# Small matmuls on opposite halves or blocks of the array, issued alternately instead of in blocks

## The chip, the core and the metric

The kernel runs as one program on one core of a Trainium2 chip. The metric is the device time of one execution in microseconds. The kernel before has a median of 2231.14 us over three runs (2227.08 to 2231.18).

The engines of the core are called PE (TensorE, matrix products), DVE (VectorE), ACT (ScalarE), POOL (GpSimd) and SP (SyncE, which here only issues DMAs). A product on PE is a weight load (the stationary operand) and a matmul that streams the other operand through. An fp32 product shows up in the trace as two weight loads and two matmul instructions.

## The reference

A sequence of 256 tokens of width 1024 goes through two blocks.

```python
# first block
x = x + 0.5 * swiglu(rms_norm(x), ffn1)            # hidden width 2816
x = x + token_mixer(rms_norm(x))                   # three attention branches, gated, then w_out
x = x + 0.5 * swiglu(rms_norm(x), ffn2)
# second block
ctx_states = rwkv_context_states(h_ctx @ w_in)     # only the final states of the recurrence
mixed = (g_hy * hyena(cols) @ hy_proj + g_rw * rwkv(cols, ctx_states) @ rw_proj) @ w_out
x = x + gate1 * rmsnorm(mixed)
x = x + gate2 * rmsnorm(expert_choice_moe(h2))     # 16 experts of width 2048, 32 tokens each
```

The recurrence is RWKV-7 with 8 heads of 64, run once forward and once backward in time:

```python
def step(S, inp):
    sa = einsum('bhij,bhj->bhi', S, a_t)
    S = S * w_t[:, :, None, :] + sa[..., None] * b_t[:, :, None, :] + v_t[..., None] * k_t[:, :, None, :]
    y = einsum('bhij,bhj->bhi', S, r_t)
```

The first of the attention branches (A) has 12 heads of 64 in 3 groups of 4; head h of the three groups shares one softmax. The third (C) selects keys by an index score, a sum over 8 small heads of relu(q . k) times a weight.

## The kernel before, in words

**Products.** The weights of the projections are split in two parts (`wsplit`: line 245 on ACT makes the high part, line 246 on DVE the low part, lines 270 to 272 do it in three engines for part of the second mixer), and each projection is three fp32r products per block (lines 287 to 289, 299 to 302, 345 to 349). The small products, which the change is about, are fp32 and not split.

**Order.** Nothing orders PE's stream by hand around the change. The kernel is traced as straight code; a planner with a model of the engines then lays out each engine's instructions, earlier code first among what it holds to be ready, and hands out the buffers of the tile pools. A read and a write of the same PSUM bank are kept apart in the order of the source. Each engine then runs its instructions in that fixed order. PSUM is split in `psM` (4 banks), `psT` (2, tiles named `tr`) and `psX` (2, tiles named `px`).

**Two halves.** A tensor with a contraction of 64 sits on partitions 0 to 63 or 64 to 127, and a product on it uses the upper or the lower half of the array's rows; an output that goes to partitions 0 to 63 or 64 to 127 uses one half of its columns.

**The recurrence** (`rwkv`, lines 921 to 1247) is called twice: by `context_states` for the context (final states only, while the first FFN and the attention's projections run) and by `mixer2` for the tokens (while the Hyena branch and the gates run). It treats chunks of 64 tokens.

- `elementwise(n, d, t)`, four times per call (direction d, token tile t): two low-rank products into a psX bank each, line 1010 on rows 0 to 63 of `up` and line 1017 on rows 64 to 127, four of 64x128 each, each bank followed by four tanh on ACT (1013, 1020).
- `products(d, t)`: line 1076 (into psX, masked by DVE line 1078), lines 1095 and 1098, whose loop alternates the row halves with each head, and line 1106, four products of `kt` and `vt` for each of the two chunk halves `cc`, each into its own psT bank, followed by copies on ACT (1110).
- The inverses of unit triangular 32-blocks are made on DVE (1131 to 1133) and travel through DRAM (`sc2`, `TC`). Then the off-diagonal blocks: lines 1162 and 1170, 64 products of 32x32 each, ordered block by block (two directions times two chunks); the second reads the copy `Bs` of the first's bank.
- The steps (lines 1197 to 1243), four per call, each for both directions. Direction d works on rows r, one half of the partitions; the other direction always has the other half. Line 1212: four products of the state with K = 128 and 64 columns into `pu`; 1214 (DVE) makes `u`; 1220: eight of 64x64 into `pz`; 1222 (ACT) copies to `z`; 1228: four of 64x128 into a psX bank for each direction; 1231 (DVE, two per direction) makes the new state; 1236 and 1240, in the second call only, add four and eight products to the output banks `psY`. Each of these loops is over the direction outside and over the heads inside, so all products of one direction come in a block.

**Attention.** `attn_c` (592) makes the index score, two heads per psX bank, bank by bank. `attn_a` (673) goes head by head; head h has the row half h % 2, its three groups go one at a time into a psX bank, and DVE adds the bias and takes the maximum. `swept` gives each head's `output` after the next head's `logits`.

**After it.** The second mixer ends with `rw_proj` and `w_out` (lines 1541 to 1543). Then the expert weights (403 MB, line 1764) stream through a ring of buffers that the earlier stages' pools have given back.

Of the kernel before, what the change touches and what calls it, by code (L numbers as in the profile page):

```python
# [11 lines left out]
F32 = mybir.dt.float32  # L12
# [153 lines left out]
def _body(nc, tc, ctx, A, out):  # L166
# [42 lines left out]
    def rsqrt(ss, p, n, eps, op=ALU.add, pool=None):  # L209
        """1/sqrt(ss + eps) (or of max(ss, eps)) on [p, n]; ss may come in two parts to add."""  # L210
# [25 lines left out]
    def mean_sq_halves(x_ap, junk):  # L236
        """The mean square of a row in two parts, for rsqrt."""
# [10 lines left out]
    def transposes(dst_fn, src, n, dense=True):  # L248
        """PE-transpose n 128-column blocks of src; dst_fn(j0, k, ps) takes each bank's worth."""
# [27 lines left out]
    def proj_tok(hT, w, kc, n0, n):  # L277
        """[128 tok, n] x 2 token tiles of h @ w[:, n0:n0+n]."""
# [13 lines left out]
    def proj_feat_acc(o, parts, hT, k0, bank0):  # L292
        """Accumulates feature-major products into o(c); the first to touch a bank starts it."""
# [11 lines left out]
    def proj_feat(hT, w, n0, n, take):  # L305
        """Feature-major [128 f, 256 tok] chunks of h @ w[:, n0:n0+n], n <= 512; take(c, ps)."""
# [14 lines left out]
    def norm_T(hT, t, x, xn, gain_bc):  # L321
        """rms norm of one token tile with a gain row, transposed and split in two parts into hT."""
# [107 lines left out]
    def attention(xs, hT, next_gain):  # L430
        """The block on the normed input hT; returns the normed input of the next, of gain next_gain."""
        with ExitStack() as fx:
# [147 lines left out]
            def bias_of(t, h, nk):  # L580
                return bias[:, h, 0:256] if t else bias[:, h, 128:256]
# [1315 lines left out]
```

## Time and profile before

| | us |
|---|---|
| median of three runs | 2231.14 |
| span of the profiled execution (first to last instruction) | 2224.2 |
| PE busy | 1826.4 (82%) |
| PE weight loads busy | 1108.2 (50%) |
| DVE busy | 887.3 (40%) |
| ACT busy | 589.9 (27%) |
| POOL busy | 335.4 (15%) |

The page gives no own time for the profiled execution besides its span; what lies around the span is the 6.9 us between it and the median. Busy time on PE counts a matmul from its start to the modelled end of its pipeline, so a busy PE is not a PE at its peak, and instructions that overlap are counted once. Shares are averages over the whole span; the kernel has two very unlike parts, so they have to be read by stage.

### The profile page before, as it was taken

Reading aid. Unit: us, or ns where it says so; the run is one execution under the profiler, and the core shown is the slowest. Engines: PE = TensorE matmul, PEld = TensorE weight load, DVE = VectorE, ACT = ScalarE, POOL = GpSimd, SP = SyncE. Lnnn points to the kernel's source line nnn. Section 1 sums busy time; section 2 is a strip of 40 time slices with the busy share of each in tenths; the row PEclk is TensorE's granted clock in tenths of the full one; section 3 lists DMA queues with packets and bytes.
Section 4 is the critical chain, followed back from the end, with each engine's and each line's share of the span. In section 5 each row is a group of like instructions: output and inputs, shape, how many; then the busy total and the mean of one; then the engine's idle time right before and its main releaser. Section 6 shows DMA issues by size and latency. Waiting matters only on the chain.

```text
span 2224.2 us, 28420 instructions
## 1 busy us (share of the span) xinstructions
PE 1826.4 (82%) x11441; PEld 1108.2 (50%) x11442; DVE 887.3 (40%) x1611; ACT 589.9 (27%) x954; POOL 335.4 (15%) x332
## 2 busy tenths in 40 slices
PE   7999999999988899898999876766766666667775
PEld 5888877777768877888687521111111111111111
DVE  4577855865757765777647410000000000000001
ACT  3345443544436544453314200000000000000001
POOL 2111013210325540235233200000000000000000
PEclk9999989999989999989889887677677787777667
DMA  8654545444448855424336899999999999999997
GB/s 296 222 167 134 171 131 171 136 145 121 132 143 270 280 185 182 141 81 113 115 105 220 314 409 410 410 409 406 407 407 406 407 407 410 410 411 409 406 407 302
DMA packets 237046, 600.95 MB, mean 270 GB/s; under 512 B 35384, under 2 KB 91217, under 8 KB 204146
## 3 DMA queue, kind: packets, MB, share of 16 engines
q1 hardware_dynamic: 200464, 551.89, 67.6%
q0 software_dynamic: 10496, 36.08, 4.9%
q10 hardware_dynamic: 25954, 11.16, 1.9%
q8 instruction: 90, 1.47, 0.3%
q14 instruction: 42, 0.34, 0.0%
HBM read 593.25 MB, written 9.75 MB: 271 GB/s over the span
## 4 chain that ended last, share of the span: by engine, by line
DMA 42%; PE 41%; DVE 8%; ACT 3%; issue 3%; POOL 1%; SPq 0%; ACTq 0%; DVEq 0%; POOLq 0%
DMA ring<-exp_w 39%; PE mm L302 4%; PE mm L299 3%; PE mm L288 3%; PE mm L301 3%; PE mm L287 3%; PE mm L289 3%; DVE wl L246 2%; PE mm L346 2%; PE mm L345 2%; PE mm L349 2%; PE px L1779 1%; DMA wraw<-w_in 1%; ACT wh L245 1%; PE tr L1812 1%
## 5 line engine op out<-in xcount | busy, mean ns | idle before, releaser
L1779 PE MATMUL px<-ring,xeT 128*32 128x512 f32 x2048 | 370.0, 812 | 181.9 <-DMA ring<-exp_w 181.7
L246 DVE TENSOR_TENSOR wl<-wraw,wh 128x1024 fp32r<-128x1024 f32 (+2 forms) x243 | 317.5, 1307 | 174.2 <-ACT wh L245 169.9
L245 ACT ACTIVATE wh<-wraw 128x1024 fp32r<-128x1024 f32 (+2 forms) x243 | 254.5, 1048 | 352.5 <-PE mm L301 143.5
L1779 PEld LDWEIGHTS px<-ring,xeT 128*32 128x32 f32 x2048 | 48.7, 123 | 474.6 <-DMA ring<-exp_w 440.4
L302 PE MATMUL mm<-hh,wl 128*128 128x256 f32 x912 | 266.6, 294 | 18.6 <-DVE wl L246 16.6
L299 PE MATMUL mm<-hh,wh 128*128 128x256 f32 x912 | 265.7, 292 | 2.1 <-ACT hh L245 2.1
L301 PE MATMUL mm<-hl,wh 128*128 128x256 f32 x912 | 264.1, 290 | 1.7 <-DVE hl L246 1.6
L1791 DVE SCALAR_TENSOR_TENSOR mth<-mth,px 128x512 f32<-128x512 f32 x16 | 11.0, 687 | 580.4 <-ACT mth L1790 580.4
L1812 PE MATMUL tr<-ring,hid 128*32 128x512 f32 x1024 | 166.8, 758 | 77.8 <-DMA ring<-exp_w 65.1
L302 PEld LDWEIGHTS mm<-hh,wl 128*128 128x128 f32 x912 | 178.6, 196 | 33.2 <-DVE wl L246 21.4
L299 PEld LDWEIGHTS mm<-hh,wh 128*128 128x128 f32 x912 | 179.6, 197 | 11.4 <-issue 7.6
L301 PEld LDWEIGHTS mm<-hl,wh 128*128 128x128 f32 x912 | 179.5, 197 | 6.6 <-issue 3.9
L1815 ACT ACTIVATE ye<-tr 128x512 f32<-128x512 f32 x32 | 19.1, 597 | 566.7 <-PE tr L1812 566.7
L1625 POOL TENSOR_SCALAR rsz<-ss 128x1 f32<-128x1 f32 x2 | 0.6, 302 | 952.9 <-ACT ring L1625 952.8
L288 PE MATMUL mm<-wl,hh 128*128 128x512 f32 (+2 forms) x320 | 127.9, 400 | 2.3 <-DVE wl L246 2.0
L1812 PEld LDWEIGHTS tr<-ring,hid 128*32 128x32 f32 x1024 | 26.4, 124 | 203.4 <-DMA ring<-exp_w 143.8
L289 PE MATMUL mm<-wh,hl 128*128 128x512 f32 (+2 forms) x320 | 124.6, 390 | 0.0
L287 PE MATMUL mm<-wh,hh 128*128 128x512 f32 (+2 forms) x320 | 117.7, 400 | 6.7 <-DVE wi L525 3.6
L1817 PE MATMUL mm<-ye,pgT 128*128 128x512 f32 x128 | 92.8, 865 | 24.0 <-ACT ye L1815 24.0
L1792 DVE SCALAR_TENSOR_TENSOR mth<-mth,px 128x512 f32<-128x512 f32 x16 | 11.0, 687 | 253.0 <-PE px L1779 253.0
L1790 ACT ACTIVATE mth<-px 128x512 f32<-128x512 f32 x16 | 9.5, 597 | 283.5 <-PE px L1779 283.5
L1817 PEld LDWEIGHTS mm<-ye,pgT 128*128 128x128 f32 x128 | 30.1, 260 | 88.4 <-ACT ye L1815 63.7
(756 smaller groups left out, 2792.4 us busy)
## 6 DMA issues: line engine op xcount, KB each, us to landing
ring<-exp_w SPq DMA_DIRECT2D x384, 1024.0 KB
wraw<-w_in SPq DMA_DIRECT2D x107, 512.0 KB
mraw<-mod_w POOLq DMA_DIRECT2D x48, 512.0 KB, 5.1
wraw<-ffn_w_gate SPq DMA_DIRECT2D x44, 512.0 KB
wraw<-ffn_w_up SPq DMA_DIRECT2D x44, 512.0 KB
wraw<-ffn_w_down SPq DMA_DIRECT2D x44, 512.0 KB
wraw<-w_out SPq DMA_DIRECT2D x11, 512.0 KB
skew<-bd POOLq DMA_DIRECT2D x1, 3840.0 KB, 27.7
```

What stands on the lines that cost most here:

```text
L245: S.activation(dst_h, src, AF.Copy)
L246: (eng or V).tensor_tensor(dst_l, src, dst_h.bitcast(F32), op=ALU.subtract)
L287: PE.matmul(ps[t], hh[:, k, sl], wh, start=(k == 0), stop=False)
L288: PE.matmul(ps[t], hh[:, k, sl], wl, start=False, stop=False)
L289: PE.matmul(ps[t], hl[:, k, sl], wh, start=False, stop=(k == kc - 1))
L299: PE.matmul(o(c), wh[:, cs], hh[:, k, :], start=(k == 0 and bank0(c)), stop=False, skip_group_check=True)
L301: PE.matmul(o(c), wh[:, cs], hl[:, k, :], start=False, stop=False, skip_group_check=True)
L302: PE.matmul(o(c), wl[:, cs], hh[:, k, :], start=False, stop=(k == KC - 1), skip_group_check=True)
L345: PE.matmul(acc[t][nh], fh[:, sl], wh[:, ns], start=(k == 0), stop=False)
L1779: PE.matmul(ps[32 * g:32 * g + 32, :], xeT[:, k, es], wt[:, 0, g * 512:(g + 1) * 512], start=(k == 0), stop=(k == KC - 1), skip_group_chec ...
L1812: PE.matmul(pe2[32 * g:32 * g + 32, :], hid[:, q, 32 * g:32 * g + 32], w2t[:, g, :], start=(q == 0), stop=(q == 3), skip_group_check=True)
L1817: PE.matmul(acc[t][nh], pgT[:, t * 128:(t + 1) * 128], ye, start=(e == 0), stop=(e == NE - 1))
```

## The change

Six places put products on opposite halves (or different blocks) next to each other: the loop over halves, blocks or directions becomes the inner one, and the reads of the banks come after both. No product, copy or DMA is added or dropped. Comments and docstrings are removed as well, line by line, which is left out here.

```diff
@@ attn_c
-                for i in range(4):
-                    hs = (i, i + 2) if i < 2 else (i + 2, i + 4)
-                    r = slice((i % 2) * 64, (i % 2) * 64 + 64)
-                    ps = psX.tile([128, 2, 256], F32, name="px")
-                    for j, h in enumerate(hs):
-                        PE.matmul(ps[:, j, :nk], qiT[r, h // 2, sl], kiT[r, :nk], start=True, stop=True)
+                for i in range(2):
+                    pair = [psX.tile([128, 2, 256], F32, name="px") for _ in range(2)]
+                    for j in range(2):
+                        for e in range(2):
+                            r = slice(e * 64, e * 64 + 64)
+                            PE.matmul(pair[e][:, j, :nk], qiT[r, 2 * i + j, sl], kiT[r, :nk], start=True, stop=True)
...
@@ attn_a: two heads at a time
+                for h0 in (0, 2):
...
                         for g in range(3):
+                            pair = [psX.tile([128, 512], F32, name="px") for _ in range(2)]
+                            for e in range(2):
+                                r = slice(e * 64, e * 64 + 64)
+                                PE.matmul(pair[e][:, :nk], aqT[r, (g * 4 + h0) // 2, sl], akT[r, (g * 4 + h0) // 2, :nk],
+                                          start=True, stop=True)
+                            for e in range(2):
+                                V.tensor_tensor_reduce(lgs[e][:, g * nk:(g + 1) * nk], pair[e][:, :nk],
+                                                       bias_of(t, g * 4 + h0 + e, nk), 1.0, GONE, ALU.add, ALU.max,
+                                                       accum_out=mxs[e][:, g:g + 1])
...
@@ elementwise
-            ps = psX.tile([128, 4, HT], F32, name="px")
+            psw, psa = [psX.tile([128, 4, HT], F32, name="px") for _ in range(2)]
             for p in range(4):
...
+                for ps, r in ((psw, slice(0, 64)), (psa, slice(64, 128))):
+                    PE.matmul(ps[:, p, :], c["up"][r, d, p * 128:(p + 1) * 128], zl[r, sl], start=True, stop=True,
+                              skip_group_check=True)
+            for ps, dst, nm in ((psw, thw, "hw0"), (psa, tha, "ha0")):
+                for p in range(4):
+                    S.activation(dst[:, p, :], ps[:, p, :], AF.Tanh, scale=0.5,
+                                 bias=c[nm][:, d * 4 + p:d * 4 + p + 1])
@@ products: the second half's bank now comes from psX
+            pk = [psT.tile([128, 4, 128], F32, name="tr"), psX.tile([128, 4, 128], F32, name="px")]
+            for p in range(4):
+                hs = slice(p * 128, p * 128 + 128)
+                for cc in range(2):
+                    r = slice(cc * 64, cc * 64 + 64)
+                    PE.matmul(pk[cc][:, p, :], kt[r, hs], vt[r, t, hs], start=True, stop=True, skip_group_check=True)
...
@@ off-diagonal blocks (the second loop likewise)
-        for d, fr, gr, gc in blocks():
-            for t in range(2):
-                for hh in range(8):
-                    q = t * 8 + hh
+        for t in range(2):
+            for hh in range(8):
+                q = t * 8 + hh
+                for d, fr, gr, gc in blocks():
                     PE.matmul(ps[gr, q, :], W[t, d][fr, hh // 4, hh % 4, 0, gc],
...
@@ step: both directions at each stage
-                    for p in range(4):
+                for p in range(4):
+                    for d, t, r in where:
                         PE.matmul(pu[r, p * 128:p * 128 + 128], AR[t, d][:, p, 0, r], ev(S_[d][:, p]), start=True,
                                   stop=True, skip_group_check=True)
+                for d, t, r in where:
                     V.tensor_tensor(u[r], pu[r], MV[d][r, t, :], op=ALU.add)
             pz = psT.tile([128, 512], F32, name="tr")
+            for h in range(8):
+                hs = slice(h * 64, h * 64 + 64)
+                for d, t, r in where:
+                    ur = u[r] if S_ is not None else MV[d][r, t, :]
+                    PE.matmul(pz[r, hs], W[t, d][r, h % 2, h // 2, 0, :], ur[:, hs], start=True, stop=True,
+                              skip_group_check=True)
             for d, t, r in where:
+                S.activation(z[r], pz[r], AF.Copy)
+            Sn = ring[step % 2]
+            pn = [psX.tile([128, 4, 128], F32, name="px") for _ in range(2)]
+            for p in range(4):
+                hs = slice(p * 128, p * 128 + 128)
+                for d, t, r in where:
+                    PE.matmul(pn[d][:, p, :], TB[d][r, t, hs], z[r, hs], start=True, stop=True, skip_group_check=True)
...
             if emit:
+                for p in range(4):
+                    for d, t, r in where:
+                        PE.matmul(psY[t][r, p * 128:p * 128 + 128], AR[t, d][:, p, 1, r], ev(S_[d][:, p]),
+                                  start=False, stop=False, skip_group_check=True)
                 for h in range(8):
                     hs = slice(h * 64, h * 64 + 64)
+                    for d, t, r in where:
                         PE.matmul(psY[t][r, hs], W[t, d][r, h % 2, h // 2, 1, :], z[r, hs], start=False,
                                   stop=False, skip_group_check=True)
```

## Rows read from the trace of the kernel before

**Rows 1.** The page's slices: PE busy in tenths, and what DMA moved.

```profile
PE   7999999999988899898999876766766666667775
...
GB/s 296 222 167 134 171 131 171 136 145 121 132 143 270 280 185 182 141 81 113 115 105 220 314 409 410 410 409 406 407 407 406 407 407 410 410 411 409 406 407 302
```

**Rows 2.** Stretches: length, busy PE, PEld, DVE, ACT, POOL; granted clock, DMA share, GB/s.

```profile
460.00:540.00 80.00, 80.00 (x385) 60.15 (x384) 46.85 (x131) 33.52 (x51) 4.59 (x3) 1.00 0.41 120
945.00:1036.00 91.00, 82.91 (x932) 75.29 (x932) 64.78 (x91) 44.64 (x99) 40.42 (x37) 0.92 0.34 93
1104.00:1182.00 78.00, 78.00 (x557) 64.73 (x558) 35.46 (x60) 17.04 (x24) 21.45 (x28) 0.89 0.29 95
```

**Rows 3.** Waits of SP's queue, 1190 to 1320 us: total, times, longest.

```profile
SPq L1764 <- PE mm L1543: 24.1, 7, 8.6
```

**Rows 4.** Timeline of PE, products in blocks: start, length, line, shapes, count.

```profile
182.11 1.16 PE L1106 MATMUL tr<-vt,kt 64*128 64x128 f32 x8
...
348.75 1.14 PE L1220 MATMUL tr<-uu,nb 64*64 64x64 f32 x16
...
1298.38 1.98 PE L1817 MATMUL mm<-ye,pgT 128*128 128x512 f32 x4 [0.72 <-ACT ye L1815]
```

**Rows 5.** Timeline of PE, products that alternate between halves.

```profile
74.84 1.05 PE L831 MATMUL px<-mraw,sc 128*32 128x512 f32 x4
...
178.29 1.03 PE L1095 MATMUL tr<-vt,nkv 64*64 64x64 f32 x28
...
180.59 0.27 PE L1010 MATMUL px<-zl,wup 64*128 64x128 f32 x1
180.69 0.27 PE L1017 MATMUL px<-zl,wup 64*128 64x128 f32 x1
180.70 0.27 PE L1010 MATMUL px<-zl,wup 64*128 64x128 f32 x1
```

**Rows 6.** Groups by line on PE: busy us, mean ns, idle before.

```profile
L1228 PE MATMUL px<-zk,tb 64*128 64x128 f32 x128 | 20.3, 304 | 0.0
L1106 PE MATMUL tr<-vt,kt 64*128 64x128 f32 x128 | 19.7, 295 | 0.0
...
L673 PE MATMUL px<-akT,aqT 64*128 64x128 f32 (+1 forms) x48 | 13.7, 371 | 0.0
L1170 PE MATMUL px<-nb,Bs 32*32 32x32 f32 x256 | 10.9, 218 | 0.0
L1240 PE MATMUL mm<-zk,nb 64*64 64x64 f32 x128 | 10.6, 245 | 0.0
```

**Rows 7.** Line 1220 alone, 145 to 1182 us: PE busy, PEld busy.

```profile
145.00:1182.00 1037.00, 19.09 (x256) 16.84 (x256) 0.95 0.50 151
```

**Rows 8.** Line 1212 alone, the same stretch.

```profile
145.00:1182.00 1037.00, 15.97 (x112) 12.68 (x112) 0.95 0.50 151
```

**Rows 9.** Line 1236 alone, the same stretch.

```profile
145.00:1182.00 1037.00, 9.64 (x64) 7.73 (x64) 0.95 0.50 151
```

**Rows 10.** Line 1162 alone, the same stretch.

```profile
145.00:1182.00 1037.00, 10.04 (x256) 9.46 (x256) 0.95 0.50 151
```

**Rows 11.** Tile wup (lines 1010 and 1017), the same stretch: PE, PEld, POOL.

```profile
145.00:1182.00 1037.00, 17.31 (x128) 15.50 (x128) 1.33 (x2) 0.95 0.50 151
```

**Rows 12.** Timeline of PE in a recurrence step of the second mixer.

```profile
1125.45 0.65 PE L1236 MATMUL mm<-S__10207,ar 128*64 128x128 f32 x4
...
1126.90 1.14 PE L1220 MATMUL tr<-uu,nb 64*64 64x64 f32 x16
1127.97 0.65 PE L1236 MATMUL mm<-S__10207,ar 128*64 128x128 f32 x4
...
1130.61 1.14 PE L1220 MATMUL tr<-uu,nb 64*64 64x64 f32 x16
```

**Rows 13.** Timeline of ACT and DVE: one copy z, one addition u.

```profile
1150.54 0.59 ACT L1222 ACTIVATE zk<-tr 64x512 f32<-64x512 f32 x1 [4.40 <-PE tr L1220]
...
1160.01 0.69 DVE L1214 TENSOR_TENSOR uu<-tr,MV 64x512 f32<-64x512 f32 x1 [2.94 <-PE tr L1212]
```

More of the change, by code (lines that the diff above doesn't have):

```diff
@@ L664, in attn_a, with logits @@
                 heads = []
-                for h in range(4):
-                    def logits(h=h):
-                        lg = tmp.tile([128, 768], F32, name="lgs", bufs=LGS)[:, :3 * nk]
-                        mx = small.tile([128, 3], F32, name="mx3")
+                for h0 in (0, 2):
+                    def logits(h0=h0):
+                        lgs = [tmp.tile([128, 768], F32, name="lgs", bufs=LGS)[:, :3 * nk] for _ in range(2)]
+                        mxs = [small.tile([128, 3], F32, name="mx3") for _ in range(2)]
@@ new lines, in logits @@
+                            for e in range(2):
+                                V.tensor_tensor_reduce(lgs[e][:, g * nk:(g + 1) * nk], pair[e][:, :nk],
+                                                       bias_of(t, g * 4 + h0 + e, nk), 1.0, GONE, ALU.add, ALU.max,
+                                                       accum_out=mxs[e][:, g:g + 1])
+                        got = []
+                        for e in range(2):
+                            m1 = small.tile([128, 1], F32, name="mx")
+                            V.tensor_reduce(m1, mxs[e], axis=AX.X, op=ALU.max)
+                            got.append((h0 + e, lgs[e], softmax(lgs[e], m1)))
@@ L683, in output @@
+                        return got
+                    def output(got):
                         kt = nk // 128
[L684 to L685 removed]
+                        for h, lg, ri in got:
+                            po = psX.tile([128, 512], F32, name="px")[:, :64]
+                            pv(lg, 3 * kt, lambda j: av[:, j % kt, ((j // kt) * 4 + h) * 64:((j // kt) * 4 + h) * 64 + 64], po)
+                            V.tensor_scalar(oA[t][:, h * 64:h * 64 + 64], po, ri, None, op0=ALU.mult)
@@ L1167, in rwkv @@
         ps = psX.tile([128, 16, 32], F32, name="px")
-        for d, fr, gr, gc in blocks():
-            for q in range(16):
+        for q in range(16):
+            for d, fr, gr, gc in blocks():
                 PE.matmul(ps[fr, q, :], Bs[gr, q, :], W[q // 8, d][gr, q // 4 % 2, q % 4, 0, gc], start=True, stop=True,
@@ new lines, in rwkv @@
+            for d, t, r in where:
+                S.activation(z[r], pz[r], AF.Copy)
[6 more added lines that the diff above has]
+            for d, t, r in where:
+                for e in range(2):
+                    f = slice(e * 64, e * 64 + 64)
+                    V.tensor_tensor(Sn[d][f, :, e, :], pn[d][f, :, e * 64:e * 64 + 64],
+                                    se[f, d] if S_ is not None else KV[d][f, step], op=ALU.add)
@@ L1222, in rwkv @@
-                S.activation(z[r], pz[r], AF.Copy)
-            Sn = ring[step % 2]
-            for d, t, r in where:
-                ps = psX.tile([128, 4, 128], F32, name="px")
-                for p in range(4):
-                    hs = slice(p * 128, p * 128 + 128)
-                    PE.matmul(ps[:, p, :], TB[d][r, t, hs], z[r, hs], start=True, stop=True, skip_group_check=True)
-                for e in range(2):
-                    f = slice(e * 64, e * 64 + 64)
-                    V.tensor_tensor(Sn[d][f, :, e, :], ps[f, :, e * 64:e * 64 + 64],
-                                    se[f, d] if S_ is not None else KV[d][f, step], op=ALU.add)
@@ L1233, in rwkv @@
-            if emit:
-                for d, t, r in where:
-                    for p in range(4):
-                        PE.matmul(psY[t][r, p * 128:p * 128 + 128], AR[t, d][:, p, 1, r], ev(S_[d][:, p]),
-                                  start=False, stop=False, skip_group_check=True)
-                    for h in range(8):
-                        hs = slice(h * 64, h * 64 + 64)
+                    for d, t, r in where:
                         PE.matmul(psY[t][r, hs], W[t, d][r, h % 2, h // 2, 1, :], z[r, hs], start=False,
```

49 lines of the change are left out of this document (9 added, 40 removed).

## The prediction

> **What bounds the kernel now.** I read the page's slices first [rows 1]. The kernel has two stages. Up to about slice 22 TensorE (PE) is busy nine tenths of the time and DMA moves 81 to 296 GB/s. From slice 23 to the end DMA moves 406 to 410 GB/s without a break while PE falls to six or seven tenths: the expert weights set the pace there, and nothing that the change touches lies in that stage.
>
> The busy time by stage came second [rows 2]. In the stretch at 460 to 540 us (attention) and in that at 1104 to 1182 us (the recurrence of the second mixer) PE is busy all of the time, and VectorE (DVE), the next, 46.9 of 80 and 35.5 of 78 us. So PE's queue ends last there: a microsecond less of PE work lets everything behind it start a microsecond sooner. At 945 to 1036 us (the second mixer's elementwise part and its products) PE is busy 82.9 of 91 us and DVE 64.8: PE already waits for other engines, and less PE work is paid only in part.
>
> Third, the waits of the DMA queue. The expert loads (line 1764) wait for buffers that the first stage frees, for instance 24.1 us in all for the matmuls of line 1543 [rows 3]. So the stream starts when that stage gets out of the way, and a shorter first stage moves the whole end, one for one. At 410 GB/s the stream has no slack of its own to take such a gain away.
>
> **What one alternation is worth.** Every fp32 product here is two instructions on PE. Today the small ones run in blocks on one half of the array: 16 instructions of 64x64 (line 1220) take 1.14 us and 8 of 64x128 (line 1106) 1.16 us; 4 of 128x512 on the whole array (line 1817) take 1.98 us [rows 4]. Less the tail of the last (about 0.22 and 0.27 us) and the slower first, that is about 58 and 112 ns from start to start. The trace also has the alternated form. Line 1095 in the context alternates row half and column half with each product: 28 instructions in 1.03 us, that is (1.03 - 0.22) / 28 = 29 ns each. Where lines 1010 and 1017 happened to overlap, two instructions of opposite row halves with all 128 columns start in each 0.11 us (180.59, then 180.69 and 180.70), 55 ns each instead of 112. And line 831, all 128 rows with two column groups, puts four instructions with 512 columns to stream in 1.05 us, where line 1817 needs 1.98; it bears on lines 1212 and 1236, which alternate column halves under all rows [rows 5]. So the full price of an alternated pair is half of the block form, for all three kinds.
>
> What the changed lines cost now, in us of PE's busy time: 1228 20.3, 1106 19.7, 673 13.7, 1170 10.9, 1240 10.6 [rows 6], 1220 19.1 [rows 7], 1212 16.0 [rows 8], 1236 9.6 [rows 9], 1162 10.0 [rows 10], and 1010 with 1017, by their weight tile, 17.3 [rows 11]: 147.2 us. Half of it, 73.6 us, is the most that alternation can take off PE. No product, copy, DMA or byte is added or removed. Line 592 (4.4 us) is left at nothing: its blocks are so short that today's order overlaps them partly; the ends are 1 us lost and 1 us won.
>
> **How much of it comes about.** An order in the source is not yet an order on the engine. PE's stream is planned, and the rows show that it goes by what is ready: at 1125.45 four instructions of line 1236 go out, then eight of 1212 and sixteen of 1220, which stand before them in the source, and at 1127.97 the other four [rows 12]. So two halves alternate only if their inputs are there together. I sort the lines by that.
>
> (a) Both halves ready together. Line 1170 reads one copied tile (Bs); line 1240 comes after 1228 and both z are done; line 1162 has its blocks of one direction at once, though the other direction's TN1 comes later, and two blocks are enough to halve. Half of 10.9 + 10.6 + 10.0 is 15.8 us. Line 1106 has one input, kt, for both halves, but its two banks now come from two pools, so I take three quarters of its half: 7.4 us. Together 23.2 us; the ends are 8 us (1170 and 1162 half of theirs, nothing else) and 25.6 us.
>
> (b) The second half becomes ready one operation later. In a recurrence step the two u are made one after the other on DVE (0.69 us each, line 1214), the two z on ACT (0.59 us each, line 1222) [rows 13]. A half of line 1220 takes 1.14 us, so 1.14 - 0.69 = 0.45 us of it overlaps with its partner, about a fifth of the pair's 2.28 us; two blocks that now stand together also change the array's layout once less. I take a quarter for lines 1220, 1228, 1212, 1236 and, where the second psX buffer comes free later than the first, for 1010, 1017 and 673: a quarter of 96.0 us is 24.0 us. The ends are nothing and a half, 48.0 us.
>
> Sum on PE: 23.2 + 24.0 = 47.2 us. Of this some 6 us lie in the stretch 945 to 1036 us (half of line 1106's 7.4 and half of the 4.3 of lines 1010 and 1017, which run for the context and for the second mixer alike), where PE waits already; I count half of it, so 3 us go: 44.2 us. Against it stand the new waits. In a step, z of the first direction waits for the second direction's products too, since pz is filled for both before it is read, and u likewise. Behind those waiting ACT and DVE instructions stand weight splits, for which PE's filler products wait. Eight steps with about 0.5 us each (a pair of line 1220 at three quarters, 1.7 us, against the 1.14 us of one half) cost 4 us; below, nothing, because today the second direction's products already come after the read of the first from the same bank (line 1220's blocks at 1126.90 and 1130.61, 3.7 us apart [rows 12]); above, 8 x (0.69 + 0.59) = 10 us. That leaves 40.2 us.
>
> The profile shows its span, 2224.2 us; the median of the runs, 2231.1, is 6.9 us (0.3%) above, which I carry over unchanged. 2231.1 - 40.2 = 2190.9, so 2191 us.
>
> A rule speaks against part of this. By line 1095's row its two halves, which write opposite partitions of one bank, start 29 ns apart on average [rows 5]. The Trainium skill, "TensorEngine Tiling (Array Packing)", section "Restrictions and Gotchas", says that different row tiles write to different PSUM banks and cannot access the same bank at the same time. By that rule lines 1162, 1170, 1220 and 1240, which write one bank for both halves, would stay serial, and the sum would lose 15.8 + 4.8 = 20.6 us. This trace does not agree with it.
>
> **Rivals.** *Full alternation.* The plan keeps the source's order, since PE is so full that by the time it gets to a step both halves are ready. For it: PE never idles at 1104 to 1182 us, and the two blocks of line 1220 wait behind projections. Against it: the split of line 1236 [rows 12]. It gives 73.6 us less 4.6 (half of what would be won in the stretch where PE waits: a quarter of line 1106's 19.7 and of the 17.3 of lines 1010 and 1017), 69 us: 2162 us.
>
> *Readiness undoes it.* Group (b) wins nothing, and of group (a) lines 1162, 1170 and half of 1106 come through: 10.5 + 5 us, 2216 us. For it the two staggers [rows 13]; against it, that blocks which merely stand next to each other overlap at their border, as at 180.59 [rows 5].
>
> *One bank, one writer.* Lines 1162, 1170, 1220 and 1240 stay serial within a bank, as the banks are shared in the new order as well; 40.2 - 20.6 = 19.6 us remain: 2212 us. This is the rule named above; line 1095 speaks against it.
>
> *The gain doesn't reach the stream.* The row of rows 3 names PE alone; if buffers whose last reader is another engine come free as late as before, the stream starts as before: 2230 us. Against it [rows 3]: the largest wait for the first stage is for PE, and the others are fed by what PE finishes.
>
> *Slower: both psX buffers taken at once.* The new order takes two banks of psX, which has two, in 8 elementwise parts, 8 recurrence steps and 12 pairs of heads, and one more in 8 products. The place is line 1076 and the output products, which need psX too: each pair makes them wait for one more release of 0.6 to 0.7 us (the nearest rows, a copy and an addition out of a bank [rows 13]): 36 x 0.65 = 23 us. It decides if PE has nothing else ready in those waits and group (b) wins nothing: 2231 + 23 - 10 = 2244 us. Against it: PE has projections to fill with in all of these stages [rows 2].
>
> **How the numbers follow.** The forecast 0.47 (its own range 2176 to 2206), full alternation 0.17, readiness 0.16, one bank 0.03, not reaching the stream 0.08, slower 0.09. The first four are faster than 2231.1 by over 0.2% (4.5 us, about what a measurement of this kernel can tell from no change): 0.83. Within it 0.08, slower 0.09. The granted clock, 0.89 and 0.92 in the two stretches of the second mixer [rows 2], may fall elsewhere than before; a few us either way. For 8 in 10 the range runs from 2157 (full alternation with a little luck) to 2228; outside lie the slower case, part of the no-change one and a little below.
>
> **What would show it.** Right: lines 1170, 1162 and 1240 at about half of their busy time; line 1220 and 1228 at three quarters; the first expert loads that wait for the first stage some 40 us sooner; the last stage as long as before. Wrong: these lines with x16 blocks as before and their time unchanged (readiness), new idle time of PE before line 1076 behind DVE line 1078 (psX), or a shorter first stage with the stream's start unmoved. The size is wrong if (b) comes out far from a quarter.

## The result, and the profile after

The kernel after takes 2190.84 us (median of four runs, 2187.64 to 2195.16); the kernel before took 2230.41 us beside it. The ratio is 0.9832 with a 95% interval of 0.9813 to 0.9850. In a second sitting, beside nine runs of before, it was 0.9848 (0.9817 to 0.9880). By these ratios the change makes the kernel faster by 34 to 38 us (the medians alone differ by 39.6 and 30.5 us), and the predicted 2191 us is the time that came out.

Line numbers move a little: 673 is 675 now, 1010 and 1017 are 1019, 1106 is 1109, 1162 is 1167, 1170 is 1175, 1212 is 1218, 1220 is 1227, 1228 is 1236, 1236 is 1245, 1240 is 1250, and the expert loads are line 1774. Below I keep the numbers of before and add the new one where a row has it.

The page's slices of the kernel after, PE in tenths and DMA in GB/s, answer to [rows 1]:

```profile
PE   7999989999988999998898877766666676666765
...
GB/s 300 224 171 149 160 138 190 138 142 127 132 170 264 292 157 200 127 105 107 92 155 264 347 406 406 410 411 410 408 407 406 407 407 407 410 411 411 409 406 278
```

The stream of expert weights runs at the same 406 to 411 GB/s, and the slice ahead of it moves 347 where it moved 314. The first stage got shorter, the second did not. Three stretches show how: to the second mixer's first low-rank product, from there to the last product of the recurrence, and from there to the first expert product. By the first expert product I mean line 1750's, now 1760, which gathers the tokens for the experts; the first product on expert weights (1779, now 1789) starts 3.3 us behind it in both kernels. First before, then after (length, busy PE, PEld, DVE, ACT, POOL; granted clock, DMA share, GB/s):

```profile
0.00:949.60 949.60, 887.52 (x5858) 746.50 (x5859) 630.72 (x1161) 433.30 (x658) 220.13 (x214) 0.97 0.57 178
949.60:1179.40 229.80, 215.10 (x1926) 180.73 (x1926) 150.51 (x247) 80.86 (x152) 82.71 (x84) 0.90 0.36 105
1179.40:1258.90 79.50, 65.35 (x304) 53.92 (x303) 54.53 (x103) 33.30 (x64) 26.94 (x26) 0.84 0.78 283
```

```profile
0.00:931.10 931.10, 868.34 (x5857) 728.69 (x5858) 631.25 (x1161) 433.41 (x658) 221.16 (x214) 0.97 0.59 181
931.10:1141.90 210.80, 187.83 (x1931) 154.84 (x1930) 148.50 (x245) 81.08 (x152) 80.59 (x84) 0.94 0.40 115
1141.90:1225.40 83.50, 66.93 (x301) 54.91 (x299) 53.75 (x105) 32.83 (x64) 27.40 (x26) 0.83 0.72 268
```

Up to the first expert product PE is busy 1123.1 us in place of 1168.0, 44.9 us less, with the same instructions. Its idle time there rises from 90.9 to 102.3 us (1258.9 - 1168.0 and 1225.4 - 1123.1). So 33.5 us reach the first expert product; from there to the end of the span it takes 968.0 us, before 965.3. The two spans therefore differ by 30.8 us only. The profiled execution of after took 2195.16 us, 1.8 us more than its span and the longest of its four; with the same 1.8 us added, that of before took 2226.0 us, less than each of its four. The granted clock is 0.95 on average up to the first expert product in both profiles, so it isn't what made the difference there.

On the changed lines (592 left out) PE's busy time falls from 147.2 to 99.4 us. Rows of the second mixer show the three kinds of outcome: four blocks interleaved (1170, now 1175), two halves interleaved (1220, now 1227), and two halves that still come as blocks (1228, now 1236). Start, length, line, shapes, count:

```profile
1077.80 1.29 PE L1175 MATMUL px<-nb,Bs 32*32 32x32 f32 x128
...
1101.98 1.15 PE L1227 MATMUL tr<-uu,nb 64*64 64x64 f32 x32
1106.52 1.16 PE L1236 MATMUL px<-zk,tb 64*128 64x128 f32 x8
1107.61 0.44 PE L1250 MATMUL mm<-zk,nb 64*64 64x64 f32 x4
1107.98 0.37 PE L1236 MATMUL px<-zk,tb 64*128 64x128 f32 x1
```

32 instructions of 64x64 now take what 16 took [rows 4]; eight of 64x128 take what eight took. Line 1228 keeps its blocks in all four steps of the second mixer; in the context three of its four steps do run in pairs, and one of these takes no longer than a block of eight:

```profile
346.55 1.16 PE L1236 MATMUL px<-zk,tb 64*128 64x128 f32 x16
```

The same by line, busy us, mean ns, idle before:

```profile
L1236 PE MATMUL px<-zk,tb 64*128 64x128 f32 x128 | 18.9, 313 | 1.1 <-ACT zk L1230 1.1
...
L675 PE MATMUL px<-akT,aqT 64*128 64x128 f32 (+1 forms) x48 | 10.2, 375 | 0.0
...
L1250 PE MATMUL mm<-zk,nb 64*64 64x64 f32 x128 | 8.4, 247 | 0.0
```

Against [rows 6]: 20.3, 13.7 and 10.6 us.

### The profile page after: what moved, and what is told of

It reads as the page before. It is cut to its first block, busy times and chain, and to the rows that moved or that the text cites. A ratio compares the mean times of both kernels' runs of the same rounds, so it can differ in the third digit from the quotient of the medians.

```text
span 2193.4 us, 28407 instructions
## 1 busy us (share of the span) xinstructions
PE 1784.5 (81%) x11441; PEld 1067.1 (49%) x11442; DVE 884.9 (40%) x1611; ACT 589.9 (27%) x954; POOL 334.8 (15%) x332
## 4 chain that ended last, share of the span: by engine, by line
DMA 43%; PE 39%; DVE 9%; ACT 3%; issue 3%; POOL 2%; SPq 0%; ACTq 0%; DVEq 0%; POOLq 0%
DMA ring<-exp_w 38%; PE mm L302 4%; PE mm L301 3%; PE mm L299 3%; PE mm L287 3%; PE mm L288 3%; PE mm L289 3%; DVE wl L246 2%; PE mm L346 2%; PE mm L349 2%; PE mm L345 2%; PE px L1789 2%; PE tr L1822 1%; DMA wraw<-w_in 1%; ACT wh L245 1%
## 5 line engine op out<-in xcount | busy, mean ns | idle before, releaser
L1789 PE MATMUL px<-ring,xeT 128*32 128x512 f32 x2048 | 365.5, 806 | 182.6 <-DMA ring<-exp_w 182.4
L302 PE MATMUL mm<-hh,wl 128*128 128x256 f32 x912 | 266.7, 294 | 16.1 <-DVE wl L246 15.1
L1822 PE MATMUL tr<-ring,hid 128*32 128x512 f32 x1024 | 175.0, 791 | 76.7 <-DMA ring<-exp_w 64.0
L1825 ACT ACTIVATE ye<-tr 128x512 f32<-128x512 f32 x32 | 19.1, 598 | 573.2 <-PE tr L1822 573.2
```

Source lines behind the costliest of these rows:

```text
L302: PE.matmul(o(c), wl[:, cs], hh[:, k, :], start=False, stop=(k == KC - 1), skip_group_check=True)
L1789: PE.matmul(ps[32 * g:32 * g + 32, :], xeT[:, k, es], wt[:, 0, g * 512:(g + 1) * 512], start=(k == 0), stop=(k == KC - 1), skip_group_chec ...
L1822: PE.matmul(pe2[32 * g:32 * g + 32, :], hid[:, q, 32 * g:32 * g + 32], w2t[:, g, :], start=(q == 0), stop=(q == 3), skip_group_check=True)
```

## Experiments

Times in different sittings are compared through the ratio to the kernel before, which ran beside each of them; its medians were 2226.0, 2227.6 and 2223.6 us. A ratio's 95% interval stands behind it.

### Each part alone

The kernel before with one part of the diff each, the hunks as shown ahead of the prediction: the off-diagonal blocks, the steps, the elementwise products with line 1106, attention (both of its places).

**Off-diagonal blocks.**

> The kernel before (2230.4 us) with one part of the change alone: the two loops of off-diagonal blocks (lines 1162 and 1170) go through the blocks inside and the heads outside. In the kernel after the two lines together take 14.2 us less of PE than before (20.9 to 6.7 us). Theory 1, what leaves PE leaves the end, because PE's queue ends last in both stages in which the loops run: the same 14 us less on these lines here, and 2216 to 2220 us. Theory 2, the wait for the second direction's TN1, on which PE now stands after its first instructions, gives most of it back: the same busy time of the lines, but 2224 to 2230 us.

**Steps.**

> The kernel before (2230.4 us) with the recurrence steps of the change alone (all five loops of a step). In the kernel after the lines of a step take 18.4 us less of PE than before (1212 5.8, 1220 8.3, 1228 1.4, 1236 0.7, 1240 2.2 us). Theory 1, what leaves PE leaves the end: 2210 to 2215 us. Theory 2, a step is a chain from one direction's products over DVE or ACT to the next products, and the merged reads lengthen it by up to 1.3 us for each of 8 steps: 2220 to 2226 us.

**Elementwise and line 1106.**

> The kernel before (2230.4 us) with two parts of the change alone: the elementwise products (lines 1010 and 1017, two psX banks) and line 1106 with its second bank from psX. In the kernel after these take 11.7 us less of PE than before (1106 9.1, 1010 and 1017 2.6 us). Theory 1, they lie half in the context, where PE sets the pace, and half where PE waits for DVE: some 5.9 us of the first half and half of the second reach the end: 2220 to 2224 us. Theory 2, taking psX banks two at a time delays line 1076, which needs the same two banks: 2228 to 2235 us.

**Attention.**

> The kernel before (2230.4 us) with the two attention parts of the change alone (lines 592 and 673). Line 673 takes 3.5 us less of PE in the kernel after. Theory 1, the 3.5 us go to the end: 2226 to 2228 us. Theory 2, two psX banks taken at once and two heads' softmax before the next pair delay the output products and the rest of the branch, so that the part costs what it saves: 2229 to 2234 us. In the kernel after the attention's last logits end 21.4 us sooner than before but the next milestone behind them only 15.8 us, which speaks for theory 2.

Measured; the last three columns are worked out from the stretches up to the first expert product, as above:

| part alone | ratio | us | PE busy | PE idle | first expert product |
|---|---|---|---|---|---|
| blocks | 0.9964 (0.9952 to 0.9977) | -8.0 | -16.1 | +3.4 | -12.7 |
| steps | 0.9970 (0.9951 to 0.9989) | -6.7 | -18.0 | +10.2 | -7.8 |
| elementwise, 1106 | 0.9955 (0.9939 to 0.9971) | -10.0 | -9.3 | +2.0 | -7.3 |
| attention | 0.9985 (0.9967 to 1.0003) | -3.3 | -3.4 | -2.3 | -5.7 |
| sum of the four | | -28.0 | -46.8 | +13.3 | -33.5 |
| kernel after | 0.9832 (0.9813 to 0.9850) | -37.5 | -44.9 | +11.4 | -33.5 |

By the start of the expert products the parts add up. That they do so to the tenth is luck: each figure is from one profile, and two profiles of the kernel after differ by 1.7 us there. In whole time they add to 28.0 us; each has an interval of 3 to 4 us to either side, so that this differs less from 34 to 38 us than it seems, and I read nothing into the rest.

The steps are the part whose saving on PE is paid worst: 18.0 us of work, 10.2 us of new idle time. The time, 6.7 us less, lies within the 4 to 10 that theory 2 of that run expected, but most of the new idle time is not in the steps. In those of the second mixer PE is busy all the time (64.1 of 64.1 us); in those of the context its waits are 3.6 us, where before has 1.4. The largest single one comes behind them: line 287 waits 7.3 us for DVE's line 525, before 3.6. So work taken off PE was in good part lost to inputs that were not ready yet, and the longer chain of a step is not shown to be the cause. Elementwise (10.0 us) and attention (3.3 us) agree with their theory 1, though the interval of attention reaches past no change. The blocks came out between the two theories in time, 8.0 us, and on theory 1 by the first expert product.

### Is it the alternation, or the merging of the two directions?

In the new steps both directions' products also come ahead of both reads of the shared bank. This kernel has that and keeps the blocks; the rest is as in the kernel before. Shown against the alternated steps:

```diff
-            for h in range(8):
-                hs = slice(h * 64, h * 64 + 64)
-                for d, t, r in where:
+            for d, t, r in where:
+                for h in range(8):
+                    hs = slice(h * 64, h * 64 + 64)
...
                     PE.matmul(pz[r, hs], W[t, d][r, h % 2, h // 2, 0, :], ur[:, hs], start=True, stop=True,
```

The loops of lines 1212, 1228, 1236 and 1240 likewise.

> The steps of the kernel after in all but one thing, the rest as in the kernel before: both directions' products at each stage stand ahead of both reads of the bank, but the products go direction by direction, in blocks, not alternately. Theory 1, the saving is the overlap of two halves on the array: line 1220 stays near its 19.1 us and 1212 near 16.0 us, less some 0.3 us for each border at which two blocks now touch (8 pairs: 2 to 3 us in all), and the time is 2224 to 2230 us. Theory 2, the saving is that no read of the shared bank stands between the two directions any more: these lines at their times in the kernel after (10.8 and 10.2 us), and a time within 3 us of the kernel with the alternated steps.

It took 0.9980 (0.9964 to 0.9996) of before, 4.5 us less, against 6.7 us less with alternation. The intervals overlap, so time doesn't tell them apart; a time that close is what theory 2 expected. PE's rows do tell them apart, and they speak for theory 1. Line 1220 (1222 in both kernels) over both calls, 145 to 1182 us (PE busy, PEld busy), first this kernel, then the alternated steps alone:

```profile
145.00:1182.00 1037.00, 15.55 (x256) 14.32 (x256) 0.96 0.51 153
```

```profile
145.00:1182.00 1037.00, 10.78 (x256) 8.99 (x256) 0.95 0.50 153
```

Of the 8.3 us that line 1220 loses from its 19.1 [rows 7], 3.5 come from putting the two blocks together and 4.8 from the alternation. For line 1212 it is 2.6 and 3.7 of 6.3 us. I had expected 0.3 us for each border at which two blocks touch, and it is 0.44 (3.5 us over 8 pairs). One pair in this kernel:

```profile
1123.43 1.90 PE L1222 MATMUL tr<-uu,nb 64*64 64x64 f32 x32
```

32 instructions in blocks take 1.90 us, alternated 1.15, and in two separate blocks 2 x 1.14. The starts inside this row are 58 ns apart behind the first gap of 106, except for eight at the border, four of either block, which start in pairs (6, 52, 54, 5, 54, 4, 54 ns). So neighbouring blocks overlap by some four instructions without being asked to; the rest takes alternation in the program.

Whether the alternation of the steps also reaches the end, these two runs don't show. The second mixer's steps take 64.1 us alternated, 69.4 in blocks and 75.8 before. But the first expert product comes 7.8 us ahead of before with alternation and 8.0 with blocks: the stretch ahead of the inverses took 135.8 us in the profile of the alternated steps and 124.2 in the other, at a granted clock of 0.89 and 0.96.

### Why line 1228 kept its blocks: one copy of z

```diff
-            for d, t, r in where:
-                S.activation(z[r], pz[r], AF.Copy)
+            S.activation(z, pz, AF.Copy)
```

> The kernel after (2190.8 us) with one copy of all 128 partitions from pz to z in place of two of 64 (line 1231 of it), so that both directions' z are ready in the same moment. Theory 1, lines 1228 and 1240 of before (1236 and 1250 of after: 18.95 and 8.40 us) kept their block form because the second z came 0.6 us after the first: they now alternate and fall to about 10.5 and 5.5 us, and the time falls by 6 to 11 us, to 2180 to 2185 us. Theory 2, the two products' banks come free one after the other (psX), and that keeps the blocks: 1236 stays at 18 to 19 us and the time within 3 us of the kernel after; 1250, which needs no psX bank, falls to about 5.5 us in either case.

Theory 1 holds. The time is 0.9787 of before (0.9765 to 0.9809), and lines 1235 and 1249 fall to 10.0 and 4.6 us (by line: busy us, mean ns, idle before):

```profile
L1235 PE MATMUL px<-zk,tb 64*128 64x128 f32 x128 | 10.0, 297 | 1.6 <-ACT zk L1229 1.6
...
L1249 PE MATMUL mm<-zk,nb 64*64 64x64 f32 x128 | 4.6, 221 | 0.0
```

The copy of twice as many partitions takes the same time, and after it both lines run in pairs:

```profile
1081.96 0.60 ACT L1229 ACTIVATE zk<-tr 128x512 f32<-128x512 f32 x1 [2.69 <-PE tr L1227]
...
1082.61 1.23 PE L1235 MATMUL px<-zk,tb 64*128 64x128 f32 x16 [0.70 <-ACT zk L1229]
...
1083.77 1.15 PE L1249 MATMUL mm<-zk,nb 64*64 64x64 f32 x32
```

So the stagger of 0.59 us between two copies [rows 13] is what kept the blocks. Once more, beside the kernel after:

> The kernel with one copy of z once more, beside the kernel after on the same chip. Its lines 1235 and 1249 fell to 9.98 and 4.59 us (from 18.95 and 8.40), PE's work before the first expert product is 17.2 us less than in the kernel after, PE's idle time there 5.9 us more, and the time was 10.3 us less, across two sittings. Theory 1, that is the kernel's own: 8 to 12 us less than the kernel after here. Theory 2, part of it is the granted clock of the steps (1.00 in its profile, 0.92 in that of after): 4 to 8 us less.

2181.06 us (2180.22 to 2183.52) against 2193.11 (2186.16 to 2193.41) for the kernel after, 12.1 us less; across the two sittings the ratio to before is 0.9787 and 0.9802. It is faster than both kernels of this case. The steps of the second mixer run at a granted clock of 1.00 in its profile in both sittings, 0.92 in both of the kernel after, so that this share of the gain came twice. It is not shown to follow from the copy: a kernel with two copies and one bank from another pool, below, has 1.00 there too.

The kernel after in that sitting:

> The kernel after once more, beside the three that follow, so that they can be compared with it on one chip. Theory 1, its time is a property of the kernel: a ratio of 0.981 to 0.985 to the kernel before and 2187 to 2195 us, and a first expert product within 4 us of 1225.4 us. Theory 2, a good part of its 39.6 us is luck of where the granted clock falls, since the four parts alone gave 8.0, 6.7, 3.3 and 10.0 us, 28 us in all: a ratio of 0.986 to 0.990.

0.9848 (0.9817 to 0.9880), 33.8 us less, first expert product at 1223.7 us: within what theory 1 expected, at the upper end of its ratios, and the profile repeats stage by stage within 2.5 us. The interval reaches into theory 2's ratios.

### Also u in one operation

On top of one z, DVE makes u for both directions with one addition of 128 partitions; for that MV is kept by step.

```diff
-            S.activation(MV[d][:, t, :], ps, AF.Copy)
+            for cc in range(2):
+                r, st = slice(cc * CH, cc * CH + CH), (2 * t + cc if d == 0 else NCH - 1 - 2 * t - cc)
+                S.activation(MV[st // 2][r, st % 2, :], ps[r], AF.Copy)
...
-                for d, t, r in where:
-                    V.tensor_tensor(u[r], pu[r], MV[d][r, t, :], op=ALU.add)
+                V.tensor_tensor(u, pu, MV[step // 2][:, step % 2, :], op=ALU.add)
```

> The kernel with one copy of z, and u made by one addition of 128 partitions for both directions in place of two of 64; for that MV is kept by step, not by token tile, and its four copies out of PSUM per call become eight of half the partitions. Theory 1, the chain of a step ends in what makes u: 0.6 to 0.7 us less in each of 6 steps that have this addition, less 2 us for the longer copies, and line 1227 nearer to 9.5 us than its 11.2: 2176 to 2179 us. Theory 2, PE has other work during the steps (idle 1.6 us in those of the second mixer), so a shorter chain buys nothing: within 2 us of the kernel with one z.

Both theories fail. In this kernel line 1220 is the state's product (before 1212), 1228 that of u (before 1220), 1236 that of z (before 1228), and 1240 makes the new state (before 1231). Line 1228 does fall to 9.50 us (10.46 with one z alone in the same sitting), but the time is 2191.52 us (2188.45 to 2192.79), 10.5 us more than with one z alone. The first expert product comes 11.3 us later (1225.0 against 1213.7 us): about 2.4 us of it by the attention's first index product, 3.9 us between the second mixer's first low-rank product and the last inverse block (124.6 against 120.7 us), where the extra copies lie, and 5.4 us in the steps (58.6 against 53.2 us). Most of the last has a single place (PE is idle 5.2 us in the steps, 1.6 with one z alone). The row of PE's waits, and the timeline around it:

```profile
PE tr L1220 <- DVE S__10207 L1240: 4.5, 1, 4.5
```

```profile
1117.49 1.16 PE L1236 MATMUL px<-zk,tb 64*128 64x128 f32 x16
...
1119.58 2.49 POOL L1509 TENSOR_TENSOR vt<-vt,lnb 128x512 f32<-128x512 f32 x2
1120.87 0.69 DVE L1510 TENSOR_TENSOR vt<-vt,mm 128x512 f32<-128x512 f32 x1 [4.66 <-POOL vt L1509]
1121.48 0.68 DVE L1511 TENSOR_TENSOR gg<-gl,mm 128x512 f32<-128x512 f32 x1
...
1123.30 0.85 DVE L1240 TENSOR_TENSOR S__10207<-px,se 64x256 f32<-64x256 f32 x2
...
1124.21 0.69 PE L1220 MATMUL tr<-S__10207,ar 128*64 128x128 f32 x2 [4.48 <-DVE S__10207 L1240]
```

The new state (1240) could be made when 1236 ends at 1118.65. In DVE's queue it stands behind lines 1510 and 1511, and 1510 waits 4.66 us for POOL. The planner had put these lines of the output stage ahead of the step. So 4.5 of the 10.5 us went to unrelated instructions ahead in a queue; what cost the rest is not separated.

### The standstill before the second direction's TN1

```diff
-        for t in range(2):
+        for d0, t in ((0, 0), (0, 1), (1, 0), (1, 1)):
             for hh in range(8):
...
-                for d, fr, gr, gc in blocks():
+                for d, fr, gr, gc in list(blocks())[2 * d0:2 * d0 + 2]:
```

> The kernel after (2190.8 us) with the first loop of off-diagonal blocks (line 1167 of it) direction by direction again, the two blocks of one direction still alternating; all of the second loop as it is. In the kernel after PE issues the first few instructions of that loop and then stands still until the second direction's TN1 is there: 4.0, 2.2 and 1.2 us ahead of it in the second mixer, 2.8 and 1.8 us in the context. Theory 1, those standstills are lost time and go: two blocks side by side are as good as four within 2 us, and the time falls by 3 to 8 us, to 2183 to 2188 us. Theory 2, the second loop needs both directions anyway and the standstill moves there: within 2 us of the kernel after.

> The kernel with one copy of z, and the first loop of off-diagonal blocks direction by direction again. Alone that took the end of the second loop from 24.7 to 27.9 us ahead of the kernel before, and by the end of the steps it was back at 34.2 against 37.5 us, at a granted clock of 0.88 against 0.92. Theory 1, the standstill before the second direction's TN1 is lost time and what came after it was the clock: 2 to 4 us less than the kernel with one z. Theory 2, PE's other work fills in either case: within 1.5 us of it.

No gain, both times, so theory 1 fails. The first took 0.9853 (0.9831 to 0.9875), against 0.9832 and 0.9848 for the kernel after; whether it is as fast, as theory 2 had it, or some us slower, the intervals leave open. With one z it is 2181.32 us against 2181.06, theory 2. The stretch of the blocks does get shorter (22.0 to 17.1 us in the kernel after, PE idle 6.7 to 4.0 us), and the steps behind it get longer by more (63.0 to 69.5 us, with no idle time at all): what PE doesn't do while it waits, it has to do later. How much of the longer steps is that and how much the granted clock, 0.88 there in place of 0.92, isn't separated. Two blocks side by side are also not as good as four: lines 1162 and 1170 together take 8.2 us in place of 6.7. With one z it is 10.8 in place of 6.6, a part of it by the clock: 64 instructions side by side take 1.20 us at a granted clock of 1.00 (1071.51 us in the first profile), 1.92 at 0.50 (1066.89 us in the second).

### Another pool for one bank

```diff
-            psw, psa = [psX.tile([128, 4, HT], F32, name="px") for _ in range(2)]
+            psw, psa = psX.tile([128, 4, HT], F32, name="px"), psT.tile([128, 4, HT], F32, name="tr")
```

> The kernel after (2190.8 us) with the second bank of the elementwise products (line 1019 of it) from psT, not psX. There only 3 of 8 pairs alternate. Theory 1, the second psX buffer comes free later than the first, since the products before hold it: now most pairs alternate, line 1019 falls from 14.7 to about 10 us, and the time falls by 1 to 4 us. Theory 2, the two halves of its input zl become ready at different times (two operations make them): line 1019 stays at 14 to 15 us and the time within 2 us of the kernel after.

Neither theory. 2207.86 us (2202.54 to 2215.91), 0.9903 (0.9881 to 0.9925) of before: 16 us slower than the kernel after by the ratios. Line 1019 takes 17.4 us, more than the 14.7 before the edit. PE's wait for line 1081, the mask of the products, in the second mixer (940 to 1075 us; in the kernel after, 0.2 us):

```profile
PE px L1079 <- DVE nb L1081: 7.0, 4, 2.5
```

PE's idle time up to the first expert product rises from 102.3 to 114.7 us, and its busy time from 1123.1 to 1131.9 us with the same instructions (at a granted clock of 0.90 in the stretch of the second mixer, where the kernel after has 0.94). The profile is that of an execution of 2215.91 us, 8 us above the median. psT is the pool that the transposes and the products take their banks from; which of them waited for the one bank I didn't separate.

## Why the prediction was right, point by point

**PE sets the pace of the first stage: shown.** What left PE left the start of the experts, less new idle time, for the parts together and for all at once (for the parts one by one, the steps least).

**The price, half of the block form: shown for two halves, too small for four blocks.** By the rows above an alternated pair costs (1.15 - 0.22) / 32 = 29 ns per instruction at line 1227, as line 1095 had it [rows 5]. Line 1175 with four blocks takes (1.29 - 0.22) / 128 = 8 ns; I had counted on two.

**Group (a), 23.2 us: 25.5 measured, from the wrong lines.** Line 1162 saved 5.9 (predicted 5.0), 1170 8.3 (5.5), 1106 9.1 (7.4; the bank from another pool didn't cost the quarter), but 1240 only 2.2 (5.3). About 2 of line 1170's 8.3 us are the clock: before, its 128 instructions took 4.43 us in the context, at a mean granted clock of 0.85, and 6.47 in the second mixer, at 0.50; now they take 1.29 in both, at 1.00. I had put 1240 here because "both z are done" when it runs. In fact its first direction is ready one copy ahead of the second and goes out at once; with one z the line falls to 4.6 us.

**Group (b), a quarter, 24.0 us: 22.2 measured, and a quarter at one line only.** Line 1220 saved 8.3 (4.8) and 1212 5.8 (4.0), since PE's other work is ahead of them and by the time it comes to them both halves are ready. 673 saved 3.5 (3.4), 1010 and 1017 2.6 (4.3), 1228 1.4 (5.1, all of it in the context), 1236 0.7 (2.4). The quarter was a mean over lines and steps that mostly do all or nothing. It depends on whether PE arrives late (1220) or follows the copy of z at once (1228 in the second mixer). The rivals "full alternation" and "readiness undoes it" each describe some of the lines; that the sum came out, 47.7 us against 47.2, is luck: the errors of the lines cancel.

**The new waits, 4 us, and 3 us in the stretch where PE waits already: 11.4 us measured.** As a sum this was too small. In the steps themselves it was about right: PE's waits rise from 1.4 to 4.2 us in those of the context, and its idle time from nothing to 1.8 us in those of the second mixer. But the way that I named, weight splits that stand behind the copies of z and u, isn't what the trace shows. PE's waits for weight splits do rise in the context's stretch, 145 to 390 us, first before, then after (engine, line, releaser: total, times, longest):

```profile
PE mm L302 <- DVE wl L246: 1.3, 2, 0.7
```

```profile
PE mm L302 <- DVE wl L246: 3.4, 2, 2.8
...
PE mm L345 <- ACT wh L245: 1.6, 1, 1.6
PE tr L1227 <- DVE uu L1221: 1.2, 2, 0.8
PE px L1236 <- ACT zk L1230: 1.1, 1, 1.1
```

The two long ones lie ahead of the first step, whose first product starts at 308.62 us:

```profile
231.05 0.58 PE L302 MATMUL mm<-hh,wl 128*128 128x256 f32 x1 [2.83 <-DVE wl L246]
...
289.26 2.08 PE L345 MATMUL mm<-wh,fh 128*128 128x512 f32 x4 [1.58 <-ACT wh L245]
```

So there PE was ahead of the engines that feed it, and not held up by a merged read. Inside the context's steps PE waits for u and z themselves (2.3 us, the rows of lines 1227 and 1236) and for a norm (line 324, 1.9 us, before 0.5).

The context's stretch up to the attention's first index product adds 5.5 us in all. The other large rise, 5.3 us, lies in the stretch of the blocks (idle 1.5 to 6.7 us), where PE starts line 1167 and stands still; all other stretches together add 0.6 us. In the second mixer, 931 to 1079 us, that line waits:

```profile
PE px L1167 <- DVE TN L1146: 3.6, 1, 3.6
...
PE px L1167 <- DMA TC<-sc: 2.7, 2, 1.6
```

Before, line 1162 waited 0.6 us for the second direction's TN1 there and not at all for the DMA of TC. I had named the lateness of TN1 and given it no price. That this idle time isn't simply lost is shown by the runs without the standstill, which were no faster.

**The last stage as long as before: shown** within 2.7 us. Of the expert loads that wait for the first stage the first two start 38 us sooner (about 40 predicted), but the next six 31.5 to 35.7 us, and those behind them 33 to 34 us, like the first expert product. So the sign that I had named looked better on the first loads than on the stream.

**One bank, one writer: refuted.** Line 1227 writes both halves into one bank at 29 ns per instruction. The Trainium skill, "TensorEngine Tiling (Array Packing)", section "Restrictions and Gotchas", holds that different row tiles can't access the same bank at the same time. The trace does not agree where the two row halves also write different partitions; none of the changed lines has two row halves on the same partitions of a bank.

**Slower, both psX buffers taken at once:** not in this change; line 1076's waits in the second mixer fell from 4.1 to 1.5 us (those of line 1095 for the same mask operation rose from 2.8 to 4.2). That the choice of banks can cost as much as I gave this rival (13 us) the run with one bank from psT suggests, 16 us slower than the kernel after; that it does so by waits for the bank is not shown.

By the time alone the forecast is within 1 us of the first sitting. By its sum it is 3 to 6 us too optimistic: 40.2 us were predicted, 34 to 38 came. The median that it started from, 2231.1, lay above those of the later sittings. The 6.9 us that I took to lie around the span are mostly something else: where a profiled execution has a time of its own, it is 1.8 us more than the span (2195.16 and 2193.4 us in the kernel after), and the rest is the difference between one execution and the median of others.

Three small things in the working don't come out of their rows; none moves the forecast. The stream runs at 406 to 411 GB/s from slice 24 on, not 23, and the last slice has 302 [rows 1]. The lower end of group (a), 8 us, is not half of what lines 1170 and 1162 would save (5.2 us; with line 1240 it is 7.9). And the 10 us that the slower rival takes off are not worked out from anything.

## What to carry to other kernels

Products on different halves or blocks of the array overlap when they stand next to each other in the program and their inputs are there in the same moment; so look at what makes the inputs, and let one instruction over all partitions make both (one copy of z was worth 10 to 12 us more, at no cost). When PE sets the pace, count what leaves it and then take off the waits that it uncovers in the engines that feed it; here they were a quarter (11.4 of 44.9 us). A shorter chain or another pool for a bank is no gain by itself: the two such edits here lost 10 and 16 us, the first nearly half of it to unrelated instructions that stood ahead in a queue, the second with more waits of PE and a lower granted clock.

## What the hardware showed that I had not expected

- Four 32x32 blocks interleaved run at 8 ns per instruction (128 in 1.29 us), two halves of 64x64 at 29 ns.
- Two neighbouring blocks on opposite halves overlap by four instructions on either side of the border, without alternation (1.90 us for 32 instructions in place of 2.28).
- An ACT copy of 512 elements on 128 partitions takes 0.60 us, on 64 partitions 0.59; a DVE addition 0.68 and 0.69.
- How the granted clock falls over the stages repeated from one profile of a program to the next: in the steps of the second mixer 0.92 in both profiles of the kernel after and 1.00 in both with one copy of z. In the kernel after a block of eight products of 64x128 took 2.07 us at 1086.13 us, at the lower level (1.2 GHz), where the same took 1.16 at 1106.52.
